# Moving the first operand differences and weight sums of a seven-product FFN multiplication to VectorE, and the second half's norm statistics ahead of one product

## The chip, the cores and the metric

One core of a Trainium2 chip runs the program. Time is device microseconds (us) of one execution. The kernel before takes 1283.18 us, the median of 3 runs (1282.71 to 1284.1).

Engines are named as the profile names them: PE is TensorE (matmul; PEld its weight loads), DVE is VectorE, ACT is ScalarE, POOL is GpSimd, SP is SyncE, which issues the transfers. Each engine works through its own list of instructions in order; one that waits holds up everything behind it on its engine.

## The reference

One step of a decoder layer: adaLN-modulated RMS norm, input projection, a causal pooling mixer and a retention mixer, output projection with a gated residual, then a second adaLN-modulated norm, a gated MLP with a causal depthwise convolution on its gate branch, and a final norm. What matters here begins behind the output projection:

```python
    x = x + gt_m * mix

    h = rmsnorm(x, g_ffn) * (1.0 + sc_f) + sh_f
    a, b = jnp.split(h @ w_ffn_in, [D_FF], axis=-1)
    a_ext = jnp.concatenate([conv_prev.astype(a.dtype), a], axis=1)
    acc = a_ext[:, 0:L] * conv_w[0]
    for i in range(1, CONV_W):
        acc = acc + a_ext[:, i:i + L] * conv_w[i]
    f = (jax.nn.silu(acc + conv_b) * b) @ w_ffn_out
    x = x + gt_f * f
```

D_MODEL is 1024, D_FF 2816 (22 blocks of 128 columns), and there are 1024 prompt tokens and 8 decode tokens, 1032 columns in all.

## The kernel before, in words

Activations lie with features on the 128 partitions (8 blocks of them, `x2[k, t]` is block k of token half t, 516 columns) and tokens along the row. Every matmul operand is split in two fp32r parts, `hi` (a cast by ACT) and `lo` (source minus `hi`, by DVE; `split2`, lines 824 to 826, whose second line is `minus`, L822), and each product is three matmuls: hi*hi, hi*lo, lo*hi (`prod`, L949 to L951).

**The FFN's first multiplication** is done by a 2x2 scheme with seven products in place of eight. For each block f of 128 gate columns (weights `raw_a`, the quarters A11 and A12) and the 128 value columns that go with them (`raw_b`: A21, A22), the left operands are A11, A12, A22 and the sums S1 = A21+A22, S2 = S1-A11, S3 = A11-A21, S4 = A12-S2 (`fin_sum`, L1099). The right operands are the quarters of the normed activations B11, B21 (first token half, feature blocks 0 to 3 and 4 to 7) and B22 (second half), and the differences T1, T2, T3, T4. One product is 24 matmuls of 258 columns. In profiles the tiles are `pA11_0`, `pS4_0` and so on, `w_S4_0` for a split left operand, `S_0` for a sum; buffer numbers and digits are left out there (`pS<-T,w_S`).

**The stage around the change.** The output projection ends with six half products (tiles `mo`), token half 0 first. `out_evac` adds the residual (L1027, or L1030 to L1034 for half 1), squares it on ACT (L1040) and adds the square into `acc2` (L1041; DVE for the last two blocks, POOL for the others). `norm2_a(t)` sums `acc2` over partitions with 12 small matmuls (L960, tile `ss_n`) and takes the root on POOL (L965); `norm2_b(t)` spreads it with 12 more (L974) and ACT copies it (L1052). `mod2` then norms and modulates the blocks of that half (L1057 on DVE, L1058 on ACT). Half 0 gives B11 and B21, so that the products A11 and A12 of the first four f (`NLEAD`; 8 products) can run before half 1 is normed: they are the cover for the second half's norm. Their loop holds the calls `norm2_a(1)` and `norm2_b(1)`:

```python
        step(f, "A11")
        ev_u1(f, lead[:, f])
        step(f, "A12")
        if f == 0:
            norm2_a(1)
        if f == 1:
            norm2_b(1)
```

Then `mod2(k, 1)` makes B22 from blocks 4 to 7, and for each k = 0 to 3 the differences h11 = h12-h11, h12 = h22-h12 (lines 1274 and 1275) and h22-h11 (`minus`), all in place in the tile `mix_all`; the last is split into T2. The products run S4, S2, S3, S1, A22, each for f = 0 and 1 (`HELD`), then those that are left of f = 2 and 3, then all seven of f = 4 to 21. T3, T1 and T4 are split from h12, h11 and four more differences (line 1289).

POOL does the weight sums S1 to S4 of every f, the first two differences of each k, and those for T4: `nc.gpsimd.tensor_tensor`.

**What sets the order.** The kernel is written in one program order; a scheduler places each engine's instructions, so neighbours in the list of an engine may come from different lines. Buffers add waits: there are 4 PSUM pairs (`banks`), of which two hold the products `pS4_0` and `pS4_1` from their end until line 1293; 5 buffers of split left operands; 3 buffers of sums and squares (`ep`, shared by L1040's squares and L1099's sums); 4 of raw weights.

Of the kernel before, what the change touches and what calls it, by code (L numbers as in the profile page):

```python
# [14 lines left out]
ALU = mybir.AluOpType  # L15
# [108 lines left out]
def trunk_step(  # L124
# [24 lines left out]
    nc = tc.nc  # L149
# [237 lines left out]
    for bi in range(len(in_blocks)):  # L387
        if bi < HEADS:
            for _ in range(2 if bi == 0 else 6):
                p, j, half = todo.pop(0)  # L390
# [430 lines left out]
    def minus(dst, a, b):  # L821
        nc.vector.scalar_tensor_tensor(dst, a, 1.0, b, ALU.mult, ALU.subtract)  # L822
# [95 lines left out]
    def banks(name):  # L918
        return pq.tile([P, 2, 512], F32, tag="q", name=name)

    def two(v):
        return v.rearrange("p (s n) -> p s n", s=2)
# [19 lines left out]
    def prod(ps, w, bs, first, last):  # L942
        for s in range(2):
            o = ps[:, s, 0:QUART]
            cols = slice(s * QUART, (s + 1) * QUART)
            for kk, b in enumerate(bs):
                ks = slice(kk * P, (kk + 1) * P)
                end = last and kk == len(bs) - 1
                mm(o, w[0][:, ks], b[:, 0, cols], start=first and kk == 0, stop=False)  # L949
                mm(o, w[0][:, ks], b[:, 1, cols], start=False, stop=False)  # L950
                mm(o, w[1][:, ks], b[:, 0, cols], start=False, stop=end)  # L951
# [16 lines left out]
    def rms2_ps(a, nq):  # L968
        ps, r, _ = a
        for q in range(nq):  # L970
            for b in range(3):
                i = 3 * q + b
                n = min(P, QUART - b * P)
                mm(ps[:, q, b * P:b * P + n], r[:, i:i + 1].to_broadcast([P, P]), ident[:, P - n:P], start=True, stop=True)  # L974
        return ps
# [11 lines left out]
    def vt(name):  # L987
        i = vslot[0] % 16
        vslot[0] += 1
        r, h = i % 4 + 4 * (i // 8), 1 - i // 4 % 2  # L990
        return vx[:, r, h * 518:(h + 1) * 518]

    x2 = {}
# [52 lines left out]
    def norm2_a(t):  # L1046
        rms2[t] = rms2_a(acc2[:, t, 0:HALF], 2, f"n2_{t}")

    def norm2_b(t):
        ps = rms2_ps(rms2[t], 2)  # L1050
        Rm[t] = acc2[:, t, 0:HALF]
        nc.scalar.copy(two(Rm[t]), ps[:, :, 0:QUART])  # L1052

    def mod2(k, t):
        np_ = HALF - (NS if t else 0)
        v = x2[k, t]
        nc.vector.scalar_tensor_tensor(v[:, 0:np_], v[:, 0:np_], scale2[:, k, 0:1], Rm[t][:, 0:np_], ALU.mult, ALU.mult)  # L1057
        nc.scalar.activation(v[:, 0:np_], v[:, 0:np_], AF.Identity, bias=sh_f[:, k, 0:1])  # L1058
# [11 lines left out]
    def bsplit(lst, k, src, name, tag):  # L1070
        if tag in "md":
            if k % 2 == 0:
                lst[k] = (m0p.tile([P, 2, 2, HALF], F32R, tag="m", name=f"{name}_{k}") if tag == "m" else double(f"{name}_{k}"))
                lst[k], lst[k + 1] = lst[k][:, 0], lst[k][:, 1]
        else:
            lst[k] = unit(f"{name}_{k}", tag)
        split2(lst[k], src)
# [12 lines left out]
    def fin_sum(f, name):  # L1090
        if (f, name) in sums:
            return sums[f, name]
        a, b = raws2[f, 0], raws2[f, 1]
        A11, A12, A21, A22 = a[:, 0:512], a[:, 512:1024], b[:, 0:512], b[:, 512:1024]
        x0, x1, op = {
            "S1": lambda: (A21, A22, ALU.add), "S3": lambda: (A11, A21, ALU.subtract),
            "S2": lambda: (fin_sum(f, "S1"), A11, ALU.subtract), "S4": lambda: (A12, fin_sum(f, "S2"), ALU.subtract)}[name]()
        s = sums[f, name] = ep.tile([P, HALF], F32, tag="s", name=f"{name}_{f}")[:, 0:512]
        nc.gpsimd.tensor_tensor(s, x0, x1, op=op)  # L1099
        return s  # L1100

    def fin_w(f, name):
        if name[0] == "S":
            src = fin_sum(f, name)
        else:
            i = ("A11", "A12", "A21", "A22").index(name)
            src = raws2[f, i // 2][:, (i % 2) * 512:(i % 2 + 1) * 512]
        w = wblock(src, f"{name}_{f}")
        wb[f, name] = w[:, 0], w[:, 1]
# [4 lines left out]
    def add_u(dst, f, src):  # L1114
        nc.vector.tensor_tensor(two(dst), PS.pop(f)[:, :, 0:QUART], two(src), op=ALU.add)  # L1115

    def ev_u1(f, u=None):
        U[f] = (vt(f"u1_{f}") if u is None else u)[:, 0:HALF]
        nc.scalar.copy(two(U[f]), PS.pop(f)[:, :, 0:QUART])

    def ev_c11(f, a=None):
        a = Fa[f, 0] = vt(f"a{f}_0") if a is None else a
        nc.vector.memset(a[:, 0:2], 0.0)
        add_u(a[:, 2:2 + HALF], f, U[f])

    def fin_c11(f):
        conv(f, 0, Fa.pop((f, 0)))
# [5 lines left out]
    def ev_c12b(f):  # L1133
        a = Fa.pop((f, 1))
        nc.gpsimd.tensor_copy(a[:, 0:2], Ca.pop(f))
        np_ = HALF - NS
        nc.gpsimd.tensor_copy(cvp[:, f, :], a[:, np_:np_ + 2])
        nc.gpsimd.tensor_copy(cvs[:, f, :, 1], a[:, 2 + np_:2 + HALF])
        conv(f, 1, a)
        out_f(f, 1)  # L1140

    def ev_c12(f):
        ev_c12a(f)
        ev_c12b(f)
# [19 lines left out]
    def out_c21(f):  # L1164
        add_u(Bt[f, 0], f, Bt[f, 0])
        out_f(f, 0)

    def evac(f, name):
# [15 lines left out]
        elif name == "A22":  # L1184
            out_c21(f)
        elif f not in HELD:
            ev_c12(f)


    RIGHT = {"A11": B11, "A12": B21, "S2": T2, "S3": T3, "S1": T1, "A22": T4, "S4": B22}  # L1190
    HELD = (0, 1)
    order = [(f, n) for n in ("S4", "S2", "S3", "S1", "A22") for f in HELD]
    order += [(f, n) for f in range(2, NLEAD) for n in NAMES[2:]]
    order += [(f, n) for f in range(NLEAD, FT) for n in NAMES]
    todo_w = deque([(f, n) for f in HELD for n in ("S4", "S2", "S1")] + [(f, n) for n in ("S3", "A22") for f in HELD] + order[10:])

    def prep(n=1):
        for _ in range(n):
            if todo_w:
                fin_w(*todo_w.popleft())  # L1200
# [3 lines left out]
    def step(f, name):  # L1204
        PS[f] = banks(f"p{name}_{f}")
        prod(PS[f], wb.pop((f, name)), RIGHT[name], True, True)
# [36 lines left out]
    for f in range(NLEAD):  # L1243
        step(f, "A11")
        ev_u1(f, lead[:, f])
        step(f, "A12")
        if f == 0:
            norm2_a(1)
        if f == 1:
            norm2_b(1)  # L1250
        ev_c11(f, ca[f // 2][:, f % 2])
    prep(2)

    def go(n, ev=True):
        f, name = order[n]
        if n + 10 < len(order):
            fin_raw(order[n + 10][0])
        step(f, name)
        prep()
        if ev:  # L1260
            evac(f, name)

    mod2_samples()
    for k in (4, 5, 6, 7, 0, 1, 2, 3):
        if k == 0:
            for f in HELD:
                go(f)
                PS0[f] = PS.pop(f)
        mod2(k, 1)
        if k >= 4:  # L1270
            bsplit(B22, k - 4, x2[k, 1], "B22", "b")
        else:
            h11, h12, h22 = x2[k, 0], x2[k, 1], x2[k + 4, 1]
            nc.gpsimd.tensor_tensor(h11, h12, h11, op=ALU.subtract)
            nc.gpsimd.tensor_tensor(h12, h22, h12, op=ALU.subtract)
            minus(h22, h22, h11)
            bsplit(T2, k, h22, "T2", "b")
    go(2)
# [7 lines left out]
    go(6)  # L1286
    go(7)
    for j in range(4):
        nc.gpsimd.tensor_tensor(x2[j + 4, 0], x2[j + 4, 0], x2[j + 4, 1], op=ALU.subtract)
        bsplit(T4, j, x2[j + 4, 0], "T4", "c")  # L1290
    for f in HELD:
        PS[f] = PS0[f]
        ev_c12a(f)
    for f in range(NLEAD):
        fin_c11(f)
    for f in HELD:
        ev_c12b(f)
# [208 lines left out]
```

## Time and profile before

| what | value |
|---|---|
| median of 3 runs | 1283.18 us (1282.71 to 1284.1) |
| profiled execution, its own time | 1283.75 us |
| its span, first to last instruction | 1282.0 us |
| mean granted TensorE clock | 0.982 |
| busy, share of the span: PE / PEld | 96% / 94% |
| busy: DVE / ACT / POOL | 64% / 35% / 30% |
| chain that ended last: PE / DVE / POOL / DMA | 85% / 7% / 3% / 2% |

PE is busy nearly throughout. In the page's 40 slices its busy share falls below 9 tenths in slice 1, in slices 17 and 18 (some 513 to 577 us), in slice 32 and in the one before last. Busy counts an instruction from start to end, also while it stands still inside; a start of one instruction while the one before it has not ended is usual (they are pipelined), so the distance from start to start is what a list of equal instructions costs.

### The profile page before, as it was taken

To read this page: it belongs to the slowest core of one execution; us is meant where nothing else is said; L and a number is where in the kernel's file an instruction comes from. 1 tells how busy PE (TensorE), PEld (TensorE's weight loads), DVE (VectorE), ACT (ScalarE), POOL (GpSimd) and SP (SyncE) were. 2 spreads that over 40 slices of the span, in tenths; PEclk is the share of its full clock that TensorE was granted. 3 is DMA by queue.
4 is the path that set the end of the run, shared out by engine and by line. 5 is a ranking of instruction groups with operands and counts; after the bars stand their busy time and mean duration, and the time that the engine had idled before them with its cause. 6 is when DMAs were issued, how large, how long until landed. Compare 5 with 4: busy or idle time off the path is not lost.

```text
span 1282.0 us, 24007 instructions
## 1 busy us (share of the span) xinstructions
PE 1236.0 (96%) x9640; PEld 1199.7 (94%) x9640; DVE 821.0 (64%) x1647; ACT 450.8 (35%) x878; POOL 389.8 (30%) x381
## 2 busy tenths in 40 slices
PE   8899999999999999968999999999999799999996
PEld 6799999999999999868999999999999799999996
DVE  4875556465753522789778777777777766676345
ACT  4453343342423411454334333343434301122053
POOL 3441111111330011464645545454553000000033
PEclk9999999999999999889999999999999899999998
DMA  8725444444410543102412222131224623332002
GB/s 319 273 59 178 122 137 156 125 140 152 143 44 1 207 151 106 39 28 74 145 64 99 75 76 78 71 100 63 88 75 141 238 83 100 100 128 71 1 34 100
DMA packets 78079, 140.57 MB, mean 110 GB/s; under 512 B 10928, under 2 KB 50064, under 8 KB 77968
## 3 DMA queue, kind: packets, MB, share of 16 engines
q1 hardware_dynamic: 74624, 138.09, 32.7%
q8 instruction: 76, 1.25, 0.4%
q10 hardware_dynamic: 3344, 0.95, 0.3%
q14 instruction: 35, 0.29, 0.1%
HBM read 115.00 MB, written 24.01 MB: 108 GB/s over the span
## 4 chain that ended last, share of the span: by engine, by line
PE 85%; DVE 7%; POOL 3%; DMA 2%; issue 1%; ACT 1%; DVEq 0%; SPq 0%; POOLq 0%; ACTq 0%
PE z L333 7%; PE z L334 7%; PE z L335 7%; PE fo L1379 6%; PE pS L949 6%; PE pS L951 6%; PE pS L950 6%; PE fo L1381 6%; PE fo L1380 6%; PE pA L950 5%; PE pA L949 5%; PE pA L951 5%; PE mo L949 2%; PE mo L951 2%; PE mo L950 2%; PE ada_ps L237 1%
## 5 line engine op out<-in xcount | busy, mean ns | idle before, releaser
L1379 PE MATMUL fo<-fhl,whl 128*128 128x258 f32 x704 | 198.0, 290 | 9.4 <-DVE xs L1344 9.1
L333 PE MATMUL z<-h_hi,hi_in 128*128 128x384 f32 (+1 forms) x624 | 203.7, 329 | 0.6 <-ACT h_hi L361 0.6
L334 PE MATMUL z<-h_lo,hi_in 128*128 128x384 f32 (+1 forms) x624 | 199.6, 320 | 0.2 <-DVE h_lo L362 0.2
L335 PE MATMUL z<-h_hi,lo_in 128*128 128x384 f32 (+1 forms) x624 | 198.7, 319 | 0.1
L1380 PE MATMUL fo<-fhl,whl 128*128 128x258 f32 x704 | 197.4, 283 | 0.0
L1381 PE MATMUL fo<-fhl,whl 128*128 128x258 f32 x704 | 195.4, 283 | 0.0
L949 PE MATMUL pS<-T,w_S 128*128 128x258 f32 x528 | 150.8, 286 | 6.5 <-ACT T L825 4.7
L950 PE MATMUL pS<-T,w_S 128*128 128x258 f32 x528 | 150.4, 285 | 5.0 <-DVE T L822 5.0
L951 PE MATMUL pS<-T,w_S 128*128 128x258 f32 x528 | 150.1, 284 | 0.0
L1344 DVE SCALAR_TENSOR_TENSOR xs<-fo,modT,xs 128x258 f32<-128x258 f32 (+1 forms) x224 | 104.5, 480 | 68.3 <-PE fo L1381 66.1
L1379 PEld LDWEIGHTS fo<-fhl,whl 128*128 128x128 f32 x704 | 132.3, 190 | 12.3 <-DVE xs L1344 10.3
L1380 PEld LDWEIGHTS fo<-fhl,whl 128*128 128x128 f32 x704 | 134.1, 190 | 0.0
L1381 PEld LDWEIGHTS fo<-fhl,whl 128*128 128x128 f32 x704 | 132.6, 190 | 0.0
L333 PEld LDWEIGHTS z<-h_hi,hi_in 128*128 128x128 f32 x624 | 117.2, 188 | 14.8 <-issue 12.8
L1161 POOL TENSOR_TENSOR mix_all<-mix_all 128x516 f32<-128x516 f32 x44 | 63.2, 1438 | 184.6 <-DVE mix_all L1115 159.6
L334 PEld LDWEIGHTS z<-h_lo,hi_in 128*128 128x128 f32 x624 | 117.9, 189 | 1.4 <-DVE h_lo L362 1.0
L335 PEld LDWEIGHTS z<-h_hi,lo_in 128*128 128x128 f32 x624 | 117.4, 188 | 0.5 <-DVE lo_in L215 0.4
L949 PEld LDWEIGHTS pS<-T,w_S 128*128 128x128 f32 x528 | 101.1, 191 | 7.3 <-ACT T L825 4.9
L950 PEld LDWEIGHTS pS<-T,w_S 128*128 128x128 f32 x528 | 101.0, 191 | 5.5 <-DVE T L822 5.5
L825 ACT CAST w_S<-S 128x512 fp32r<-128x512 f32 x88 | 54.5, 620 | 142.3 <-PE pS L951 87.9
L951 PEld LDWEIGHTS pS<-T,w_S 128*128 128x128 f32 x528 | 101.2, 192 | 0.0
L1154 DVE SCALAR_TENSOR_TENSOR mix_all<-mix_all,pa 128x508 f32<-128x508 f32 (+1 forms) x80 | 91.2, 1140 | 7.1 <-ACT mix_all L1149 4.9
(249 smaller groups left out, 3129.8 us busy)
## 6 DMA issues: line engine op xcount, KB each, us to landing
raw_ada<-w_ada SPq DMA_DIRECT2D x64, 256.0 KB, 3.5
raw_in<-w_in SPq DMA_DIRECT2D x26, 512.0 KB, 4.2
raw_a<-w_fin SPq DMA_DIRECT2D x25, 512.0 KB, 3.6
fd<-mix_all SPq DMA_DIRECT2D x44, 258.0 KB, 2.9
raw_fo<-fd SPq DMA_DIRECT2D x22, 516.0 KB, 4.5
raw_b<-w_fin SPq DMA_DIRECT2D x22, 512.0 KB, 3.6
raw_wo<-w_fout SPq DMA_DIRECT2D x22, 512.0 KB, 4.3
x2d<-mix_all SPq DMA_DIRECT2D x16, 258.0 KB, 2.4
```

The lines of the kernel that those rows point to most:

```text
L333: mm(ps[:, 0:n], hi[:, ws], xh[:, k, 0:n], start=first, stop=False)
L334: mm(ps[:, 0:n], hi[:, ws], xl[:, k, 0:n], start=False, stop=False)
L335: mm(ps[:, 0:n], lo[:, ws], xh[:, k, 0:n], start=False, stop=last)
L949: mm(o, w[0][:, ks], b[:, 0, cols], start=first and kk == 0, stop=False)
L950: mm(o, w[0][:, ks], b[:, 1, cols], start=False, stop=False)
L951: mm(o, w[1][:, ks], b[:, 0, cols], start=False, stop=end)
L1154: nc.vector.scalar_tensor_tensor(s[:, 0:np_], a[:, i:i + np_], cw(i, f), s[:, 0:np_], ALU.mult, ALU.add)
L1161: nc.gpsimd.tensor_tensor(s, s, Bt.pop((f, t)), op=ALU.mult)
L1344: nc.vector.scalar_tensor_tensor(dst[:, 0:np_], ps[:, 0:np_], gt_f[:, m, 0:1], dst[:, 0:np_], ALU.mult, ALU.add)
L1379: mm(o, w[:, 0, ms_], v[:, 0, cols], start=i == 0, stop=False)
L1380: mm(o, w[:, 0, ms_], v[:, 1, cols], start=False, stop=False)
L1381: mm(o, w[:, 1, ms_], v[:, 0, cols], start=False, stop=i == len(fs) - 1)
```

## The change

The diff has three parts. (1) `fin_sum` for f = 0 and 1 (`FIRST`) runs on DVE. (2) All twelve in-place differences (8 in lines 1274 and 1275, 4 in line 1289) run on DVE through `minus`. (3) `norm2_a(1)` and `norm2_b(1)` stand ahead of `step(f, "A12")` of their f, no longer behind it.

```diff
         s = sums[f, name] = ep.tile([P, HALF], F32, tag="s", name=f"{name}_{f}")[:, 0:512]
-        nc.gpsimd.tensor_tensor(s, x0, x1, op=op)
+        (nc.vector if f in FIRST else nc.gpsimd).tensor_tensor(s, x0, x1, op=op)
...
-    HELD = (0, 1)
+    HELD = FIRST = (0, 1)
...
         step(f, "A11")
         ev_u1(f, lead[:, f])
-        step(f, "A12")
         if f == 0:
             norm2_a(1)
         if f == 1:
             norm2_b(1)
+        step(f, "A12")
         ev_c11(f, ca[f // 2][:, f % 2])
...
-            nc.gpsimd.tensor_tensor(h11, h12, h11, op=ALU.subtract)
-            nc.gpsimd.tensor_tensor(h12, h22, h12, op=ALU.subtract)
+            minus(h11, h12, h11)
+            minus(h12, h22, h12)
             minus(h22, h22, h11)
...
-        nc.gpsimd.tensor_tensor(x2[j + 4, 0], x2[j + 4, 0], x2[j + 4, 1], op=ALU.subtract)
+        minus(x2[j + 4, 0], x2[j + 4, 0], x2[j + 4, 1])
```

On POOL's list this takes away 20 instructions (8 sums, 12 differences); on DVE's list they appear. The scheduler also moves others. Three places:

On PE, at the sum of the second half's squares (`ss_n2_1`; one row stands for one matmul). Before, ten matmuls of A12 of f = 0 stand ahead of it:

```order
L951 MATMUL pA12_0_6180<-B21_0_5989,w_a0_5759 128x258
L949 MATMUL pA12_0_6180<-B21_2_5998,w_a0_5759 128x258 [waits Activation_49]
L950 MATMUL pA12_0_6180<-B21_2_5998,w_a0_5759 128x258 [waits DVE_49]
L951 MATMUL pA12_0_6180<-B21_2_5998,w_a0_5759 128x258
L949 MATMUL pA12_0_6180<-B21_2_5998,w_a0_5759 128x258 [waits Activation_49]
L960 MATMUL ss_n2_1_6205<-ones_93,acc2_5049 128x2 [waits DVE_49,PE_49]
L960 MATMUL ss_n2_1_6205<-ones_93,acc2_5049 128x2 x5
L949 MATMUL pA11_1_6218<-B11_0_5971,w_a1_5822 128x258 [waits PE_49]
```

and with the change it stands right behind A11 of f = 0:

```order
L949 MATMUL pA11_0_6154<-B11_2_5980,w_a0_5759 128x258
L950 MATMUL pA11_0_6154<-B11_2_5980,w_a0_5759 128x258
L951 MATMUL pA11_0_6154<-B11_2_5980,w_a0_5759 128x258
L960 MATMUL ss_n2_1_6180<-ones_93,acc2_5049 128x2 [waits DVE_49,PE_49]
L960 MATMUL ss_n2_1_6180<-ones_93,acc2_5049 128x2 x5
L949 MATMUL pA12_0_6191<-B21_0_5989,w_a0_5759 128x258 [waits PE_49,Activation_49]
```

All of A12 of f = 0 now stands behind the statistics; their second set (L974) stands ahead of A12 of f = 1, where it stood behind it.

On ACT, between the squares of the last two blocks of the second half (`sq2_6_1` and `sq2_7_1`; the second is the last thing that `acc2` waits for). Before:

```order
L1040 ACTIVATE sq2_6_1_6061<-mix_all_774 128x516
L825 CAST w_S4_0_6075<-S4_0_6073 128x512
L1058 ACTIVATE mix_all_774<-mix_all_774,modT_148 128x516
L825 CAST w_a3_5959<-raw_a3_5957 128x1024
L825 CAST B21_2_5998<-mix_all_774 128x516
L1058 ACTIVATE mix_all_774<-mix_all_774,modT_148 128x516
L825 CAST w_S2_0_6078<-S2_0_6071 128x512
L1040 ACTIVATE sq2_7_1_6135<-mix_all_774 128x516
```

and with the change:

```order
L1040 ACTIVATE sq2_6_1_6061<-mix_all_774 128x516
L1058 ACTIVATE mix_all_774<-mix_all_774,modT_148 128x516 x2
L825 CAST w_a3_5959<-raw_a3_5957 128x1024
L825 CAST B21_2_5998<-mix_all_774 128x516 x2
L1119 COPY u1_lead_6151<-pA11_0_6154 128x516
L825 CAST w_S4_0_6075<-S4_0_6073 128x512
L825 CAST w_S2_0_6078<-S2_0_6071 128x512
L825 CAST w_S1_0_6139<-S1_0_6069 128x512
L1040 ACTIVATE sq2_7_1_6135<-mix_all_774 128x516
```

The cast of the sum S4 went from ahead of the modulation (L1058) to behind both B21 casts; the last square stands behind three weight casts.

On DVE, from the evacuation of A12 of f = 2 to the split of the third T2 block. Before (L822 with `mix_all` on both sides is `minus` in place):

```order
L1115 TENSOR_TENSOR c11_1_6153<-pA12_2_6304,u1_lead_6151 128x516
L822 SCALAR_TENSOR_TENSOR B22_2_6406<-mix_all_774,B22_2_6406 128x516
L822 SCALAR_TENSOR_TENSOR B22_3_6411<-mix_all_774,B22_3_6411 128x516
L1057 SCALAR_TENSOR_TENSOR mix_all_774<-mix_all_774,scale2_150,acc2_5049 128x508
L822 SCALAR_TENSOR_TENSOR mix_all_774<-mix_all_774 128x516
L1057 SCALAR_TENSOR_TENSOR mix_all_774<-mix_all_774,scale2_150,acc2_5049 128x508
L822 SCALAR_TENSOR_TENSOR mix_all_774<-mix_all_774 128x516
L822 SCALAR_TENSOR_TENSOR T2_0_6483<-mix_all_774,T2_0_6483 128x516
L822 SCALAR_TENSOR_TENSOR T3_0_6568<-mix_all_774,T3_0_6568 128x516
L822 SCALAR_TENSOR_TENSOR T2_1_6491<-mix_all_774,T2_1_6491 128x516
```

and with the change:

```order
L1115 TENSOR_TENSOR c11_1_6153<-pA12_2_6304,u1_lead_6151 128x516
L822 SCALAR_TENSOR_TENSOR mix_all_774<-mix_all_774 128x516 x5
L822 SCALAR_TENSOR_TENSOR T2_0_6483<-mix_all_774,T2_0_6483 128x516
L822 SCALAR_TENSOR_TENSOR mix_all_774<-mix_all_774 128x516 x2
L1115 TENSOR_TENSOR c11_1_6153<-pA12_3_6357,u1_lead_6151 128x516
L822 SCALAR_TENSOR_TENSOR T2_1_6491<-mix_all_774,T2_1_6491 128x516
L822 SCALAR_TENSOR_TENSOR mix_all_774<-mix_all_774 128x516
L1057 SCALAR_TENSOR_TENSOR mix_all_774<-mix_all_774,scale2_150,acc2_5049 128x508
L822 SCALAR_TENSOR_TENSOR T3_0_6568<-mix_all_774,T3_0_6568 128x516
L822 SCALAR_TENSOR_TENSOR T2_2_6499<-mix_all_774,T2_2_6499 128x516
```

Three in-place differences for each k stand on DVE in place of one, and the convolution's steps (L1154) moved behind them.

## Rows read from the trace of the kernel before

**Rows 1.** Busy time by stretch: us, then busy us (count) by engine, granted clock, DMA share.

```profile
512.00:532.00 20.00, 16.90 (x128) 15.92 (x127) 19.85 (x30) 14.34 (x24) 6.18 (x4) 0.92 0.13 34
...
560.00:580.00 20.00, 10.29 (x58) 9.58 (x57) 18.27 (x17) 9.66 (x17) 16.05 (x12) 0.66 0.00 0
...
640.00:700.00 60.00, 60.00 (x502) 60.00 (x501) 45.34 (x64) 22.50 (x36) 31.55 (x30) 1.00 0.24 80
```

**Rows 2.** Timeline, PE: start, duration, engine, line, what; in brackets idle before, releaser.

```profile
528.77 0.58 PE L949 MATMUL pA<-B,w_a 128*128 128x258 f32 x1 [2.26 <-ACT B L825]
530.19 0.58 PE L950 MATMUL pA<-B,w_a 128*128 128x258 f32 x1 [0.84 <-DVE B L822]
...
570.78 0.58 PE L949 MATMUL pS<-T,w_S 128*128 128x258 f32 x1 [4.73 <-ACT T L825]
...
573.72 0.58 PE L950 MATMUL pS<-T,w_S 128*128 128x258 f32 x1 [2.35 <-DVE T L822]
```

**Rows 3.** Timeline, ACT, the first weight cast.

```profile
526.01 0.62 ACT L825 CAST w_S<-S 128x512 fp32r<-128x512 f32 x1 [3.00 <-POOL S L1099]
```

**Rows 4.** Timeline, POOL, the first weight sum and the third.

```profile
513.62 1.77 POOL L1099 TENSOR_TENSOR S<-raw_b 128x512 f32<-128x512 f32 x1
...
524.30 1.68 POOL L1099 TENSOR_TENSOR S<-raw_a,S 128x512 f32<-128x512 f32 x1 [7.20 <-DVE acc L1041]
```

**Rows 5.** Timeline, DVE: in-place differences and two groups of splits.

```profile
556.30 1.78 DVE L822 SCALAR_TENSOR_TENSOR mix_all<-mix_all 128x516 f32<-128x516 f32 x1 [2.55 <-POOL mix_all L1275]
...
569.59 0.69 DVE L822 SCALAR_TENSOR_TENSOR mix_all<-mix_all 128x516 f32<-128x516 f32 x1 [1.16 <-POOL mix_all L1275]
...
578.31 2.98 DVE L822 SCALAR_TENSOR_TENSOR T<-mix_all,T 128x516 fp32r<-128x516 f32 x3
...
599.13 1.44 DVE L822 SCALAR_TENSOR_TENSOR T<-mix_all,T 128x516 fp32r<-128x516 f32 x1
```

**Rows 6.** Timeline, DVE, the norms, splits and evacuations ahead of the second half.

```profile
511.94 6.38 DVE L1057 SCALAR_TENSOR_TENSOR mix_all<-mix_all,scale,acc 128x516 f32<-128x516 f32 x5 [0.58 <-ACT acc L1052]
518.24 1.29 DVE L822 SCALAR_TENSOR_TENSOR B<-mix_all,B 128x516 fp32r<-128x516 f32 x2
...
523.47 0.69 DVE L1041 TENSOR_TENSOR acc<-acc,sq 128x516 f32<-128x516 f32 x1
...
527.27 0.48 DVE L1030 SCALAR_TENSOR_TENSOR mix_all<-mo,modT,xr 128x258 f32<-128x258 f32 x1
...
528.23 1.23 DVE L822 SCALAR_TENSOR_TENSOR w_a<-raw_a,w_a 128x1024 fp32r<-128x1024 f32 x1
...
529.45 0.69 DVE L822 SCALAR_TENSOR_TENSOR B<-mix_all,B 128x516 fp32r<-128x516 f32 x1
...
546.69 2.06 DVE L1057 SCALAR_TENSOR_TENSOR mix_all<-mix_all,scale,acc 128x508 f32<-128x508 f32 x3
```

**Rows 7.** Timeline, PE, statistics of the second half, the clock's return, first S4.

```profile
531.49 2.69 PE L960 MATMUL ss_n<-ones,acc 128*128 128x2 f32 x12
...
538.89 0.29 PE L951 MATMUL pA<-B,w_a 128*128 128x258 f32 x1
...
543.70 1.39 PE L974 MATMUL ss_n<-co,r_n 128*128 128x128 f32 x12
...
556.53 0.28 PE L949 MATMUL pS<-B,w_S 128*128 128x258 f32 x1
...
562.28 0.28 PE L949 MATMUL pS<-T,w_S 128*128 128x258 f32 x1
```

**Rows 8.** Timeline, PE: two matmuls 12 apart, the first S3, the first A22 of f = 2.

```profile
574.96 0.42 PE L949 MATMUL pS<-T,w_S 128*128 128x258 f32 x1
...
577.54 0.42 PE L949 MATMUL pS<-T,w_S 128*128 128x258 f32 x1
...
582.04 0.36 PE L949 MATMUL pS<-T,w_S 128*128 128x258 f32 x1 [0.47 <-DVE u_lead L1115]
...
612.07 0.28 PE L949 MATMUL pA<-T,w_A 128*128 128x258 f32 x1
```

## The prediction

> **What bounds the kernel now.** I read busy time by stretch first. From 640 us on PE is busy in all 60 of 60 us at full clock, with DVE at 45 of them and POOL at 32 [rows 1]: nothing that the change touches there can help, and whatever reaches that stretch sooner moves the end by as much. The stage to look at is 512 to 612 us. There PE runs 16.90 of 20 us and then 10.29 of 20, at granted clocks of 0.92 and 0.66, while DVE is busy 19.85 and 18.27 of 20 [rows 1].
>
> Next, PE's idle time in that stage. It comes twice: 2.26 and 0.84 us at the first A12, waiting for B21's casts and splits, and 4.73 and 2.35 us at the first S2 product, waiting for the T2 splits [rows 2]. What do these wait for?
>
> The first: ACT stood 3.00 us before the cast of the sum S4, for POOL [rows 3], with the modulation and the B21 casts queued behind; and POOL had stood 7.20 us before it began that sum, for DVE's add of a square [rows 4], whose buffer it takes. The second: DVE waited for POOL's differences (2.55 and 1.16 us ahead of two of them) and was slow itself: the in-place difference at 556.30 took 1.78 us, the same form at 569.59 took 0.69 [rows 5]. The long ones stand beside a POOL instruction, so I read 1.1 us of each as standing still.
>
> **The change, part by part.** From start to start, two splits of 516 columns cost 0.60 each (1.29 for two with 0.69 for the last), the norm's step 0.66 (2.06 for three) [rows 6], a matmul of 258 columns 0.12 at full clock (48 from 556.53 to 562.28) [rows 7] and 0.215 at the lower one (12 from 574.96 to 577.54) [rows 8]. A moved instruction is priced as a split, 0.605: same width, two operands in SBUF.
>
> *Weight sums, up to the statistics.* Five norm steps took 6.30 up to the next start at 518.24 [rows 6], 3.3 by themselves; the other 3.0 came with three POOL instructions, two of them sums [rows 4]. Without these I take 2.0 off. The 5.23 us from there to the add at 523.47 [rows 6] stay, so the add ends at 522.05. Behind it DVE's new list has two norm steps (1.32), two sums (1.21), the residual's pieces (0.96), the last double-width split with a small piece (1.22, 528.23 to 529.45 [rows 6]), both B21 splits (1.21) and S4 (0.605): S4 is there at 528.6. ACT then casts three sums, and only then squares the last block: four times some 0.55 (0.62 each, overlapping [rows 3]) gives 530.8, and DVE's add (0.69) 531.6.
>
> *The statistics, one product sooner.* They now stand right behind the first A11, whose last matmul ends near 525.8 (six of A12 ran before the idle that ended at 528.77). So PE stands from 525.8 to 531.6, 5.8 us where it had 3.1, and the statistics begin at 531.6 instead of 531.49 [rows 7]: not sooner in time, and with ten matmuls fewer done. They take 2.7 us, to 534.3. The clock, lower after this idle as after the one before, came back at 538.89, 8.7 to 10.1 us after PE went on at 530.19 or 528.77 [rows 2, 7]; counted from 531.6 that is 540.3 to 541.7, I take 541. The 48 matmuls up to the second set then end at 543.0 (31 at 0.215, 17 at 0.12). It stood at 543.70 [rows 7], so the second half's norm starts 0.7 us sooner, but five products (14.4 us) are left behind it, not four: S4 begins at 543.0 + 1.4 + 14.4 = 558.8, against 556.53 [rows 7]. **PE is 2.3 us late here**, and this part alone would cost about that.
>
> *Twelve differences, eight of them before T2's last split.* DVE's three norm steps of 546.69 [rows 6] come at 546.0. From there to the fourth T2 split its new list holds 7 norm steps (4.6) and 28 instructions at 0.605 (16.9): 567.5. POOL's first sum for f = 2 can start then, as soon as a weight split frees its buffer, and costs DVE 1.1 more: 568.6. PE waited for this split at 573.72 [rows 2]; it comes **5.1 us sooner**. PE ends both S4 products at 564.6, does the 19 matmuls that need it not (566.9), stands 1.7 us where it stood 4.73 and 2.35, and ends both S2 products at 572.1; with no long idle the clock stays up, and no matmul behind pays 0.215. S3, at 582.04 before [rows 8], could start 9.9 us sooner.
>
> *From there DVE sets the pace.* PSUM pairs come free, and T4 is split, in DVE's order. From 568.6 to the last T4 split it has 30 instructions at 0.605 and 9 convolution steps at 0.66: 24.2, so 592.8. POOL's next five sums block it: in the trace one group of three splits took 2.98 for 1.89 (two places so, 1.1 each) and a split at 599.13 took 1.44 for 0.69 (two so, 0.75 each) [rows 5], one sum cost nothing: 3.7, so 596.5. PE has only 28 matmuls (3.4) left then, since S2 and S3 of f = 2 stand ahead in its list now; S1 of f = 2 waits for a pair that DVE frees after three convolution steps, a split and an evacuation, 3.5 with small pieces, and one POOL product blocks 1.1: 601.1. Its 24 matmuls end at 604.0, where A22 of f = 2 began at 612.07 [rows 8]: **8.1 us sooner**.
>
> The SP queue follows: the raw weights of f = 1 wait for one more write of x2d, which itself comes 2 us earlier, and are not due on PE until S4; the raws of f = 3 go out when A22's splits free them, some 10 us sooner. POOL loses 20 instructions and does its f = 2 sums sooner. Behind 612 us PE is the bound and DVE has a quarter of the time free [rows 1], so the 8.1 us stay.
>
> The profiled execution took 1283.75 us (span 1282.0), 0.6 over the median of 1283.18: 1275.65 on its own time, **1275.1 for the median**.
>
> A page of the Trainium skill speaks against the change: Perfetto Trace Analysis, section Optimizing Scalar/DVE Operations, says that where DVE is saturated some work may be given to other engines, GpSimd even; here work goes the other way, onto an engine that is busy 18 of 20 us, and by that rule 20 instructions would lengthen the stage by some 12 us. The same section adds that the two share a read port, so that a shift may not help. The rows show why busy misleads here: 1.1 of 1.78 us at 556.30 was no work [rows 5].
>
> For the size of a block, SBUF — State Buffer, section Who interferes with whom, has the later of two such instructions stand for the whole of the other; the rows have 1.1 and 0.75 us, less than a POOL sum's 1.68 [rows 4, 5]. By the page the gain would be nearer the small end below.
>
> **Bounds.** No POOL instruction hits a DVE one of two SBUF operands: 5.9 less on DVE's path, of which PE, with the waits that are left, can take some 4.9: 13.0 us sooner, 1270.2. Each of the seven blocks lasts a whole POOL sum of 1.77 [rows 4]: 12.4 instead of 5.9, 6.5 dearer, 1.6 us sooner, 1281.6.
>
> **The rivals.**
> - *Few blocks.* POOL's f = 2 sums mostly fall on evacuations, which read PSUM. For it: one of six cost nothing. Against: five did. 1270.2.
> - *The statistics come later.* ACT's last square waits behind casts that wait for DVE's sums. If the norm steps are not faster (2.0) and five sums take 1.28 each instead of 0.605 (3.4, as if POOL's pace went with them), PE stands 11.2 us, DVE starts the second half 5.4 later, and 2.7 us are left: 1280.5. Against: the add at 523.47, of the same kind, took 0.69 [rows 6].
> - *Slower: in-place differences are long by themselves.* Three of the four in the trace are like the one at 556.30 [rows 5]; if that is their own length, there is no blocking to lose, and 16 of them (12 moved, 4 old) cost 1.17 more than counted: 18.8, less the 5.9 of blocks that then do not exist: 4.8 us slower, 1288.0. It decides from 1.5 us a piece on. Against: 0.69 at 569.59 in the same form [rows 5], and splits, which are not in place, were stretched as well.
> - *It doesn't reach the end.* The lists show that the instructions move, but a wait that no row here shows, say for raw weights of f = 3, could take the gain back: no change.
>
> **How the numbers follow.** Forecast 0.58 (1272.6 to 1277.6), few blocks 0.19, later statistics 0.14, slower 0.06, given back 0.03. 0.2%, 2.6 us, is about what a measurement of this kernel can tell from no change. Faster takes the first two and half of the third, 0.84; same the other half and the last, 0.10; slower 0.06. The range goes from just under the lower bound, 1270.0, to near the upper, 1281.5; beyond it lie the slower case, part of the later statistics and a little below, some 0.18.
>
> **What would show it.** Right: PE idle of 5 to 7 us just before the statistics near 531.6; S4 at 558 to 560; the wait for T2 under 3 us; no granted clock under 0.95 in 560 to 580; in-place differences near 0.69; A22 of f = 2 at 602 to 606; the rest shifted as a block. Wrong: differences of 1.5 us and more; a statistics wait past 535; the S2 products still waiting 5 us; or a PE wait behind 612 that was not there.

## The result, and the profile after

The changed kernel takes 1273.78 us, the median of 4 runs (1273.13 to 1275.44), where the kernel before took 1283.64 on the same chip: ratio 0.9926, 95% interval 0.9909 to 0.9943. The forecast was 1275.1. The profiled execution is the quickest of the four: 1273.13 us on its own time, span 1271.3.

Busy time by stretch, to be held against [rows 1] (us, then busy us and count for PE, PEld, DVE, ACT and POOL, granted clock, DMA share, GB/s):

```profile
512.00:532.00 20.00, 13.99 (x117) 13.81 (x115) 19.47 (x37) 14.06 (x24) 1.13 (x1) 0.96 0.19 67
560.00:580.00 20.00, 19.58 (x158) 18.91 (x157) 20.00 (x31) 10.95 (x18) 11.62 (x5) 1.00 0.17 54
640.00:700.00 60.00, 60.00 (x502) 60.00 (x501) 45.40 (x63) 22.53 (x36) 31.37 (x30) 1.00 0.25 80
```

From 560 to 580 PE ran 158 matmuls at full clock; before it ran 58 at 0.66. DVE is busy in all of the 20 us, where it was busy in 18.27, and did 31 instructions where it did 17. From 640 us on PE is busy throughout, as before. The price is in the first row: 117 matmuls where there were 128.

PE's timeline, at the places of [rows 2, 7, 8] (start, duration, engine, line, what; in brackets the idle time before and who ended it):

```profile
531.77 2.69 PE L960 MATMUL ss_n<-ones,acc 128*128 128x2 f32 x12 [6.01 <-DVE acc L1041]
...
537.26 0.31 PE L950 MATMUL pA<-B,w_a 128*128 128x258 f32 x1
...
541.50 1.39 PE L974 MATMUL ss_n<-co,r_n 128*128 128x128 f32 x12
...
557.21 0.28 PE L949 MATMUL pS<-B,w_S 128*128 128x258 f32 x1
...
566.19 0.39 PE L950 MATMUL pS<-T,w_S 128*128 128x258 f32 x1 [0.42 <-DVE T L822]
...
601.62 0.28 PE L949 MATMUL pA<-T,w_A 128*128 128x258 f32 x1
```

One idle time of 6.01 us stands where B21's two waits were, just before the second half's statistics. For T2 PE stands 0.42 us. Before, it stood three times, 9.7 us in all: 4.73 and 2.35 [rows 2], and ahead of these once more, in the kernel before:

```profile
565.55 0.39 PE L950 MATMUL pS<-T,w_S 128*128 128x258 f32 x1 [2.63 <-DVE T L822]
```

A22 of f = 2 (last row of the changed kernel) begins 10.45 us sooner, and the span is 10.7 shorter.

DVE's timeline shows where the time came from; [rows 5, 6] have its rows of before (the first: 6.38 us for the same five norm steps):

```profile
511.90 4.27 DVE L1057 SCALAR_TENSOR_TENSOR mix_all<-mix_all,scale,acc 128x516 f32<-128x516 f32 x5 [0.57 <-ACT acc L1052]
...
530.93 0.69 DVE L1041 TENSOR_TENSOR acc<-acc,sq 128x516 f32<-128x516 f32 x1
...
552.68 3.10 DVE L822 SCALAR_TENSOR_TENSOR mix_all<-mix_all 128x516 f32<-128x516 f32 x5
...
565.45 3.11 DVE L822 SCALAR_TENSOR_TENSOR T<-mix_all,T 128x516 fp32r<-128x516 f32 x5
...
572.50 2.40 DVE L822 SCALAR_TENSOR_TENSOR mix_all<-mix_all 128x516 f32<-128x516 f32 x2
...
593.27 0.68 DVE L822 SCALAR_TENSOR_TENSOR T<-mix_all,T 128x516 fp32r<-128x516 f32 x1
```

Five in-place differences take 3.10 us, some 0.6 each, where single ones took 1.78 before. Of the in-place ones only the pair at 572.50 is still 1.1 too long, beside a sum of POOL. The same over the whole stretch, DVE's instructions of L822 alone (us, then DVE's busy us and count, granted clock, DMA share, GB/s); first the kernel before:

```profile
546.00:580.00 34.00, 22.41 (x21) 0.80 0.04 15
```

and the changed kernel:

```profile
546.00:580.00 34.00, 27.08 (x40) 1.00 0.10 32
```

1.07 us a piece before, 0.68 after: with nearly twice as many of these instructions DVE was busy only 4.7 us longer.

### The profile page after: what moved, and what is told of

Its sections match the earlier page's. It is cut to its first block, busy times and chain, and to the rows that moved or that the text cites. A ratio compares the mean times of both kernels' runs of the same rounds, so it can differ in the third digit from the quotient of the medians.

```text
span 1271.3 us, 23985 instructions
## 1 busy us (share of the span) xinstructions
PE 1229.9 (97%) x9640; PEld 1193.6 (94%) x9640; DVE 820.5 (65%) x1667; ACT 450.7 (35%) x878; POOL 369.6 (29%) x361
## 4 chain that ended last, share of the span: by engine, by line
PE 86%; DVE 8%; POOL 1%; DMA 1%; issue 1%; ACT 1%; DVEq 0%; SPq 0%; POOLq 0%; ACTq 0%
PE z L333 7%; PE z L334 7%; PE z L335 7%; PE fo L1379 7%; PE fo L1381 6%; PE fo L1380 6%; PE pS L949 6%; PE pS L951 6%; PE pS L950 6%; PE pA L949 4%; PE pA L951 4%; PE pA L950 4%; PE mo L949 2%; PE mo L951 2%; PE mo L950 2%; PE ada_ps L237 2%
## 5 line engine op out<-in xcount | busy, mean ns | idle before, releaser
L949 PEld LDWEIGHTS pS<-T,w_S 128*128 128x128 f32 x528 | 99.7, 189 | 2.9 <-DVE mix_all L1115 1.4
L950 PEld LDWEIGHTS pS<-T,w_S 128*128 128x128 f32 x528 | 99.7, 189 | 0.6 <-DVE T L822 0.6
L951 PEld LDWEIGHTS pS<-T,w_S 128*128 128x128 f32 x528 | 99.9, 189 | 0.0
L1154 DVE SCALAR_TENSOR_TENSOR mix_all<-mix_all,pa 128x508 f32<-128x508 f32 (+1 forms) x80 | 91.5, 1143 | 6.9 <-ACT mix_all L1149 4.8
```

What stands on the lines that cost most here:

```text
L1154: nc.vector.scalar_tensor_tensor(s[:, 0:np_], a[:, i:i + np_], cw(i, f), s[:, 0:np_], ALU.mult, ALU.add)
```

## Experiments

### The parts alone, and two of them

Three kernels make one part each: the `FIRST` line (the eight sums), the three `minus` lines (the twelve differences), and the two lines that put the statistics ahead of A12. A fourth makes the first two parts. Their diffs are pieces of the one shown above.

> Part 1 alone: the eight weight sums of f = 0 and 1 on DVE; differences on POOL and the norm calls as before. Theory A (the time comes from DVE no longer waiting for POOL's differences and no longer being stopped by them, the other two parts only move a stall about): the statistics find PE at the end of the first A12 (528.7) and still come at 531.7, a wait of about 3 us; the second set is reached near 541.5 (543.70 before), DVE's second half starts 2.2 us sooner, the POOL-paced S2 wait stays: 2 to 3 us faster, about 1281. Rival B (the gain is the statistics' earlier place on PE): no change, 1283.5. Rival C (the gain is ACT no longer standing 3.0 us before the first weight cast): 6 us or more faster, 1277.

> Part 2 alone: the twelve differences on DVE; sums on POOL and the norm calls as before. Theory A: everything as before up to the second set of statistics at 543.70; from the first norm step of the second half (545.89) to the last T2 split 22.4 us as in the changed kernel, so 568.3 in place of 573.7; PE still waits some 3.5 us for it, in one piece; A22 of f = 2 near 604 (612.07 before): about 8 us faster, 1275 to 1276. Rivals B and C: 0 to 2 us faster, 1282 to 1284. If in-place differences were long in themselves: slower, 1288.

> Part 3 alone: the two norm calls ahead of A12; sums and differences on POOL. Theory A: PE stops for 5 to 6 us behind the first A11, until the add of the last square near 531.4; the second set comes near 541.3, S4 near 557, T2 splits 2 us sooner: 0 to 2.5 us faster, 1281 to 1283.5. Rival B: nearly the whole gain, 8 to 10 us faster, 1274 to 1276.

> Parts 1 and 2 without part 3: norm calls behind A12 as before. Theory A: statistics at 531.8 as with the change, since the last square's add sets that; PE has done the first A12 by then and waits 3 us in place of 6.0; the second set at 541.5 as with the change, S4 near 554.3 in place of 557.21; but T2's last split at 566 as with the change, so PE waits there some 3.5 us and DVE sets the rest: within 1 us of the whole change, 1273 to 1275. Rival B: at least 4 us slower than the whole change, 1278 or more.

And later, the two other parts together:

> Differences by VectorE and the statistics one product sooner, the sums of f = 0 and 1 left on POOL. Theory A, parts that add up: 6.4 and 1.2 sooner than before, 1276.0, with PE standing 6 us or a little more before the statistics and under 3 us in all for the T2 splits. Rival F: with the sums on POOL the last square waits longer (POOL's sums hold the casts ahead of it on ACT) and the statistics come at 534 or later, S4 at 560: 1278 to 1279.

Measured, ratios to the kernel before in the same series. The last column is PE's stage in the one profiled execution, from the start of the first A11 to the start of A22 of f = 2; in the kernel before it is 612.07 - 522.73 = 89.34 us.

| kernel | median us | ratio, 95% interval | A11 to A22, us |
|---|---|---|---|
| sums alone | 1281.34 | 0.9984 [0.9975, 0.9994] | 87.70 |
| differences alone | 1277.10 | 0.9950 [0.9931, 0.9968] | 83.72 |
| statistics alone | 1282.68 | 0.9991 [0.9981, 1.0000] | 88.40 |
| sums and differences | 1274.46 | 0.9930 [0.9906, 0.9954] | 80.89 |
| differences and statistics | 1274.84 | 0.9936 [0.9922, 0.9949] | 80.50 |
| all three | 1273.78 | 0.9926 [0.9909, 0.9943] | 78.92 |

The differences carry the change: some 6 of its 9.5 us. Sums and statistics by themselves stay within 0.2%. Added to the differences, each seems to bring some 2 to 3 us more, in the medians and in the last column, but the intervals overlap, so this is likely and not shown. The third part brings about 1 us, which these runs can't tell from nothing: the changed kernel, run again, needed 80.74 us for the stage.

Why the sums alone bring little is plain from PE's timeline of that kernel, the S2 products:

```profile
563.96 0.39 PE L950 MATMUL pS<-T,w_S 128*128 128x258 f32 x1 [2.62 <-DVE T L822]
...
569.19 0.58 PE L949 MATMUL pS<-T,w_S 128*128 128x258 f32 x1 [4.73 <-ACT T L825]
...
572.13 0.58 PE L950 MATMUL pS<-T,w_S 128*128 128x258 f32 x1 [2.36 <-DVE T L822]
```

PE reached S4 1.6 us sooner (554.95, before 556.53), and then stood for T2 three times, each as long as before. The last of these waits ended 1.6 us sooner than before [rows 2]: the stage was shifted, not shortened. With the differences alone the same place looks like this (this execution is 1.9 us late already at the first A11):

```profile
567.90 0.39 PE L950 MATMUL pS<-T,w_S 128*128 128x258 f32 x1 [1.33 <-DVE T L822]
...
570.25 0.80 PE L949 MATMUL pS<-T,w_S 128*128 128x258 f32 x2 [1.56 <-ACT T L825]
...
571.41 0.58 PE L950 MATMUL pS<-T,w_S 128*128 128x258 f32 x1 [0.36 <-DVE T L822]
```

That is 3.3 us in three waits, as forecast (3.5), where it was 9.7. The median is 1 to 2 us above the forecast of 1275 to 1276. Part of that shows in the profile: ahead of the last T2 split two rows of DVE, at 565.52 and 567.77, are 1.1 us over their length, beside sums of POOL that the forecast did not count.

The statistics alone only move a stall, from the first A12 to the place ahead of the statistics:

```profile
531.48 2.69 PE L960 MATMUL ss_n<-ones,acc 128*128 128x2 f32 x12 [5.70 <-DVE acc L1041]
```

With that, theory A holds of the parts, to 1 or 2 us; that the gain comes from earlier statistics (rival B) or from ACT's first weight cast (rival C) falls. So does rival F: with differences and statistics the statistics begin at 530.90 and S4 at 557.63, not at 534 and 560.

### Eight subtractions by POOL that nobody waits for

The old differences could have cost DVE time in two ways: by being waited for, and by standing beside DVE's own instructions. The next kernel keeps the second and drops the first.

```diff
+    scr = sq.tile([P, HALF], F32, tag="scr", name="scr", bufs=1)
     mod2_samples()
...
             minus(h22, h22, h11)
+            for _ in range(2):
+                nc.gpsimd.tensor_tensor(scr, h12, h11, op=ALU.subtract)
```

> The whole change, and besides eight subtractions of 128x516 by GpSimd from two finished operands into a tile that nobody reads, issued where the eight differences of the T2 loop used to be issued; VectorE's list is that of the changed kernel. No engine waits for their results but GpSimd's own later work (a 2-column copy and f = 2's sums). This tells what the old differences cost by standing beside VectorE's from what they cost by being waited for. Theory A with the prediction's price (1.1 us of VectorE per GpSimd subtraction, wherever it falls): the stretch from 546 to the last T2 split grows by up to 8.8 us, the last T2 split ends at 572 to 575, A22 of f = 2 begins at 607 to 610: 1280 to 1282.5. Rival G (GpSimd stands while VectorE runs instructions with two operands in SBUF, and gets in only behind others, so it costs VectorE little, and the old kernel lost its time by waiting for results): the eight take far longer than 1.7 us each, up to 3 to 7 us, VectorE's instructions stay near 0.61 each, the last T2 split ends before 568, and the time stays within 2 us of the changed kernel's, 1273 to 1276, unless f = 2's sums get late.

Measured 1284.21 us, ratio 1.0010 [1.0001, 1.0019]: **the whole gain is gone**, with DVE's list as in the changed kernel. POOL's timeline:

```profile
557.28 10.28 POOL L1279 TENSOR_TENSOR scr<-mix_all 128x516 f32<-128x516 f32 x6
...
570.02 1.66 POOL L1099 TENSOR_TENSOR S<-raw_b 128x512 f32<-128x512 f32 x1 [1.85 <-DVE w_S L822]
571.64 3.41 POOL L1279 TENSOR_TENSOR scr<-mix_all 128x516 f32<-128x516 f32 x2
```

and DVE's beside it:

```profile
557.83 3.49 DVE L822 SCALAR_TENSOR_TENSOR mix_all<-mix_all 128x516 f32<-128x516 f32 x2
561.25 0.68 DVE L1115 TENSOR_TENSOR c<-pA,u_lead 128x516 f32<-128x516 f32 x1
561.85 1.18 DVE L822 SCALAR_TENSOR_TENSOR T<-mix_all,T 128x516 fp32r<-128x516 f32 x1
562.95 1.79 DVE L822 SCALAR_TENSOR_TENSOR mix_all<-mix_all 128x516 f32<-128x516 f32 x1
564.67 1.77 DVE L1057 SCALAR_TENSOR_TENSOR mix_all<-mix_all,scale,acc 128x508 f32<-128x508 f32 x1
566.36 2.37 DVE L822 SCALAR_TENSOR_TENSOR T<-mix_all,T 128x516 fp32r<-128x516 f32 x2
...
570.46 1.76 DVE L822 SCALAR_TENSOR_TENSOR T<-mix_all,T 128x516 fp32r<-128x516 f32 x1
572.15 1.76 DVE L822 SCALAR_TENSOR_TENSOR mix_all<-mix_all 128x516 f32<-128x516 f32 x1
573.84 1.76 DVE L822 SCALAR_TENSOR_TENSOR T<-mix_all,T 128x516 fp32r<-128x516 f32 x1
...
576.12 4.19 DVE L822 SCALAR_TENSOR_TENSOR T<-mix_all,T 128x516 fp32r<-128x516 f32 x5
```

The pair at 557.83 took 3.49 us for 1.29; a split, a norm step and a difference took 1.76 to 1.79 for 0.69 to 0.74. The evacuation at 561.25, which reads PSUM, kept its 0.68. Added up, the rows before the last are 9.1 us over their lengths, for eight subtractions and one weight sum (570.02), 1.0 each. The last T2 split, the first of the five at 576.12, ends at 576.8, 10.7 us later than in the changed kernel (566.13), 1.5 of which stood there already at the second set of the statistics (542.99, 541.50). PE waits 2.94, 3.54 and 1.01 us for these splits, its clock is 0.69 in 560 to 580, and A22 of f = 2 begins at 612.56, 0.5 us later than in the kernel before. From the last T2 split to A22 it is 35.8 us, in the changed kernel 35.5: what was lost was lost ahead of that split, on DVE, and PE's lower clock adds at most 0.3. The forecast from 1.1 us a piece was 1280 to 1282.5, which the time exceeds by 1.7: the price was right, and the 1.5 us of the second set and the one weight sum, which the forecast did not count, make up the rest. Rival G falls: here a POOL instruction nobody waits for is as dear as one that is waited for.

### The weights prepared later

The 6.0 us before the statistics are ACT's last square, behind three weight casts:

```profile
528.47 1.66 ACT L825 CAST w_S<-S 128x512 fp32r<-128x512 f32 x3 [1.89 <-DVE c L1123]
530.03 0.63 ACT L1040 ACTIVATE sq<-mix_all 128x516 f32<-128x516 f32 x1
```

The first cast begins as DVE's sum S4 ends (528.44); the profile puts its wait down to a small DVE instruction (L1123) that ended at about the same time. What the square needs was there long before, with the last piece of the residual, at 525.48:

```profile
525.33 0.15 DVE L1034 TENSOR_TENSOR mix_all<-gs_o,xr 128x8 f32<-128x8 f32 x1
```

So the preparation of these weights goes behind the first products. (The expectation names f = 1's weights; the edit moves those of both f = 0 and f = 1.)

```diff
         elif i == NTAIL + 1:
             fin_raw(1)
-            prep(2)
-    prep(2)
...
         ev_c11(f, ca[f // 2][:, f % 2])
-    prep(2)
+        if f:
+            prep(2)
```

> The whole change, and besides f = 1's weights (three sums, seven splits and casts for the first two products) are prepared three program places later, behind the A11 and A12 evacuations of f = 0 and 1. Theory A: PE's 6.0 us before the statistics are the last square waiting on ACT behind three weight casts that wait for DVE's sums. With these behind it the add of the last square ends near 526.9, PE stands about 1 us there, and its clock does not fall; the second set of ones-matmuls comes near 534.5 instead of 541.5, S4 near 549.6 instead of 557.2. Some 2.4 us of sums and splits move into DVE's second half, which sets the pace from there, so about 5 us are left at the end: 1268.8, A22 of f = 2 at 596.5, and PE stands 3 to 4 us for the T2 splits. Rival D: PE stands there for the norm itself (POOL's inverse root and the transposes) or for the DVE list in front, and the order of the weight casts does not matter: 1273 to 1275, with an idle of 5 us or more at the statistics. Rival E: DVE is the bound from 512 us on already, so what PE gains there is lost at the T2 splits to the last us: 1272 to 1275 with an idle of 8 us at S2.

> Sums and differences by VectorE, the statistics left at their old place (behind the first A12), weights of f = 1 prepared later as in the kernel beside it. Theory A: with the weight casts out of the way the last square is ready before PE ends the first A12, so there is no idle at the statistics at all; S4 near 548.4, DVE's second half starts some 2 us later than with the statistics sooner, and DVE sets the pace: 1269, within 1 us of the kernel beside it. Rival D (the casts' order does not matter): 1274 to 1275, as sums and differences alone. If placing the statistics one product sooner is worth what it is meant to be worth once its wait is gone, this one is 2 us behind the kernel beside it.

Measured: the whole change with it 1271.58 (ratio 0.9907 [0.9892, 0.9922]); without the sooner statistics 1274.16 (0.9925 [0.9913, 0.9938], single runs 1270.8 to 1275.63). PE's timeline of the first:

```profile
527.52 1.47 PE L960 MATMUL ss_n<-ones,acc 128*128 128x2 f32 x12 [1.31 <-DVE acc L1041]
...
562.40 0.51 PE L949 MATMUL pS<-T,w_S 128*128 128x258 f32 x2 [2.09 <-ACT T L825]
563.56 0.39 PE L950 MATMUL pS<-T,w_S 128*128 128x258 f32 x1 [0.65 <-DVE T L822]
```

and the last piece of the residual and the last square in the same kernel:

```profile
524.72 0.17 DVE L1034 TENSOR_TENSOR mix_all<-gs_o,xr 128x8 f32<-128x8 f32 x1
...
525.94 0.63 ACT L1040 ACTIVATE sq<-mix_all 128x516 f32<-128x516 f32 x1
```

The stall was this preparation, as theory A has it and D does not: 1.31 us are left of 6.01, and S4 begins 5.3 us sooner (551.92). Of the 4.7 us that went, 3.5 are the square's wait behind the casts (from the residual to the square 4.55 us, now 1.05). Another 1.0 comes from two sums gone from DVE's list ahead of the residual, which ends at 524.89 in an execution that is 0.45 us late at the first A11. At the T2 splits 2.6 us of the 5.3 are left, at the end 2.2: DVE, with the sums and splits now in the middle of its work, sets the pace, which is what rival E says; its sizes (nothing left, and an idle of 8 us at S2, where PE stands 2.7) were wrong. The estimate of 5 us was too high by half.

The second kernel, sums and differences without the sooner statistics, shows no gain over the same without the later weights (1274.46), and misses its forecast of 1269 by 5 us. In its profiled execution, the quickest (1270.8), the stall at the statistics is gone as well, 1.94 us without and 0.47 with the later weights; S4 begins at 549.09, but PE then stands 5.8 us for T2. The 2 us between the two kernels lie as forecast, but the second one's runs spread over 5 us, so this is weak.

To tell 2 us from chance, both were run again side by side:

> The changed kernel as it is, beside the next one on the same chip, to tell the two apart: 1273.8 as before, with its interval.

> The kernel with f = 1's weights prepared later, beside the changed kernel on the same chip. If 1271.6 was real, its ratio lies below the other's with intervals that do not overlap, 2 us or 0.17% less; if it was the spread of runs, the two lie within 1 us.

Measured: the changed kernel 1275.18 (1272.87 to 1275.77; 0.9925 [0.9912, 0.9938]), with later weights 1270.99 (1268.97 to 1273.29; 0.9898 [0.9883, 0.9912]). The intervals only touch, so the test named in the expectation is not quite met, but it was the lower one both times: the later weights are worth some 2 to 4 us more, 12 to 13 in all against the kernel before. It is the best kernel of this study.

Since DVE is its bound, f = 1's sums went back to POOL (`HELD, FIRST = (0, 1), (0,)`):

> The kernel with f = 1's weights prepared later (1271.6), and f = 1's four sums given back to GpSimd. With VectorE the bound behind 532 us, four instructions of 0.6 us leave its list: 2.4 us sooner at the T2 splits if GpSimd's sums cost VectorE nothing, 1269.2; 1271.6 again if each costs it some 0.6 us; and 1272 to 1274 if f = 1's S4 weights come too late for PE because a GpSimd sum takes 1.3 us and stands for VectorE before.

Measured 1272.66 (0.9925 [0.9912, 0.9939]): no gain, and the upper of the three values named above, but not for its reason: PE reaches S4 without a wait (552.17) and stands 4.3 us for T2 instead of 2.7. DVE's timeline has two reasons:

```profile
534.45 2.98 DVE L822 SCALAR_TENSOR_TENSOR w_S<-S,w_S 128x512 fp32r<-128x512 f32 x3
540.63 0.69 DVE L822 SCALAR_TENSOR_TENSOR w_S<-S,w_S 128x512 fp32r<-128x512 f32 x1 [3.21 <-ACT w_S L825]
...
545.91 1.78 DVE L1057 SCALAR_TENSOR_TENSOR mix_all<-mix_all,scale,acc 128x508 f32<-128x508 f32 x1
```

Three splits and a norm step stand 1.1 us each beside POOL's sums, 2.2 of the 2.4 us that the four sums had taken. And DVE stands 3.21 us for the cast of a sum that POOL made, ahead of the second half's first norm step, which comes at 541.38 instead of 538.40 (with f = 1's sums on DVE).

## Why the prediction was right, step by step

- **The norm steps, and the statistics that don't come sooner: right to 0.2 us.** The add of the block before the last ends at 522.02 (forecast 522.05), the sum S4 at 528.44 (528.6), the last square at 530.66 (530.8), its add at 531.62 (531.6), the statistics begin at 531.77 (531.6) after 6.01 us of idle PE (5.8). The moved statement looks like a gain, but for the statistics it bought nothing, and by itself the part stayed within 0.2%.
- **The clock's return: 3.7 us off in this execution.** It came at 537.26 instead of 541, so the second set began at 541.50, not 543.0, and S4 at 557.21, not 558.8. The term was taken from the kernel before and varies. When the changed kernel was run again, its statistics came 0.54 us earlier, and its profile has them so:

```profile
531.23 2.69 PE L960 MATMUL ss_n<-ones,acc 128*128 128x2 f32 x12 [6.01 <-DVE acc L1041]
...
542.14 1.39 PE L974 MATMUL ss_n<-co,r_n 128*128 128x128 f32 x12
```

With 0.54 added that is 542.68, 0.3 from the forecast; this execution took 1274.9 us. From the first set of the statistics to the second, five executions with this order took 9.73 to 11.01 us, against 11.4 in the forecast: the term was 0.4 to 1.7 us too large. S4 at 557.21 and A22 at 601.62 lie 0.8 and 0.4 us outside the ranges that the prediction named as signs, by this term and the next.
- **The T2 splits and PE's wait: right, but for one block.** The prediction read two waits at S2 where there were three, leaving out the 2.63 us; its sum goes by DVE's times, so nothing hangs on it. Forecast 568.6 with 1.1 us for POOL's first sum beside them; they end at 566.13. 1.5 of that comes from the clock, the rest from this term: the sum came, stood itself, and cost the T2 splits nothing.

```profile
562.63 7.08 POOL L1099 TENSOR_TENSOR S<-raw_b 128x512 f32<-128x512 f32 x1 [3.77 <-DVE w_S L822]
...
572.58 1.76 POOL L1099 TENSOR_TENSOR S<-raw_a,raw_b 128x512 f32<-128x512 f32 x1
```

DVE's rows of L822 keep 0.68 until its evacuation at 568.48; the split behind it, at 569.09, beside the end of that sum, is 0.5 over. So PE stood 0.42, not 1.7. The sum at 572.58 did cost its 1.1.
- **From there DVE sets the pace: right.** The last T4 split ends at 593.95, 27.8 us after the last T2 split; forecast 24.2 + 3.7 = 27.9, and the blocks in it came to 3.4. S1 of f = 2 begins at 598.65 (601.1), A22 at 601.62 (604.0): 2.4 us sooner than forecast, 1.5 for the clock and 1.1 for the block, less 0.2 elsewhere.
- **In-place differences: 0.6 us each,** so the slower rival is out. "Few blocks" is out too: from 569 to 597 us DVE's rows are 4.5 us over their lengths, in six places, though four of them cost only 0.5 to 0.7. The later statistics did not come, and nothing behind 612 us took the gain back.
- **Work taken back onto a busy engine: the stage became shorter,** by 10.45 us, and the kernel with eight idle subtractions on POOL shows that here offloaded work is paid for on DVE. The rule that work may go from a saturated engine to GpSimd (Trainium skill, Perfetto Trace Analysis, section Optimizing Scalar/DVE Operations) would, by the prediction's estimate of 20 times 0.605, have had it 12 us longer. The trace agrees with that section's other sentence, that the two engines share a read port and a shift between them might not help; that the port is the cause no run here shows by itself.
- **The size of a block: the smaller value was the better one.** 1.0 to 1.1 us a piece were measured at most, against 1.28 for a sum beside nothing and up to 1.76 for one that stood itself. The Trainium skill (SBUF — State Buffer, section SBUF: two separate sides) has the one that comes later stand for the whole of the other. A sum that took 7.08 us, through nine of DVE's instructions, does not fit that (last section).

## What to carry to other kernels

Before giving elementwise work to GpSimd beside a VectorE that is full, look at VectorE's rows beside it: where the same form takes 1.8 us in one place, beside a GpSimd instruction, and 0.7 in another, the difference may be GpSimd's, as it was here, and an instruction of 0.6 us on VectorE itself is then cheaper than one it does not have to do at all but stands still for (1.0 to 1.1). Ask of a wait that is moved what the engine that is waited for has queued ahead of it: here three weight casts ahead of one square, the first of them waiting for a sum, cost 3.5 us of the moved stall, and moving the preparation was worth some 2 to 4 us. Where a term is the time until the clock returns, give it the spread of several executions and not one value.

## What was not expected of the hardware

**How long POOL stands is uneven.** In the changed kernel a sum of 128x512, 1.28 us elsewhere, took 7.08, and a copy of 128x2 took 3.01, both beside a run of DVE's two-operand instructions that lost nothing; with the later weights f = 2's first sum took 9.55 and 9.56 in two executions. With eight idle subtractions the two engines went nearly in step instead: POOL every 1.71 us (10.28 for six), and in the three rows from 570.46 DVE every 1.69. The two long ones came after POOL had been idle (3.77 and 5.02 us); the first six subtractions came right behind a copy that had itself stood for 3.01. The length of the idle time does not tell the cases apart: the weight sum at 570.02, after 1.85 us of idle, took 1.66, and the one of 9.56 came after 1.30. What lets POOL in, in the middle of such a run or only behind it, these runs don't settle, and no kernel here was made for it.

**The clock after an idle PE differs between executions of one kernel.** Granted clock by stretch (columns as in the first view of the section on the result), in the profile of the changed kernel:

```profile
536.00:540.00 4.00, 4.00 (x30) 4.00 (x30) 3.10 (x5) 1.14 (x2) 0.60 (x2) 0.84 0.11 14
```

and in that of the changed kernel run again:

```profile
536.00:540.00 4.00, 4.00 (x23) 4.00 (x22) 3.17 (x5) 0.63 (x2) 0.00 (x0) 0.57 0.20 33
```

Both had the same 6.01 us of idle PE and then the same work; the lower level, 1.2 GHz, lasted to 537.3 in the one and to 539.3 in the other. With later weights PE stood 1.31 us in both executions, and the clock in 528 to 532 was 0.78 in one and 1.00 in the other. From the start of the statistics to the second set the two executions differ by 1.2 us without the later weights and by 1.55 us with them. Single runs of these two kernels differ by 1.7 to 4.3 us within a series, so the clock can be a good part of that spread; that it is, these runs don't show.
